# A hybrid decoder layer: half of the second output projection placed beside attention, attention's outputs loaded in 4 pieces, fill-in steps tied to an issue order

## The chip, the cores and the metric

One core of a Trainium2 chip runs the whole layer in one launch. The metric is device microseconds per execution. Engines are TensorE (PE in the profile), VectorE (DVE), ScalarE (ACT), GpSimd (POOL) and SyncE (SP), whose queue issues nearly all transfers.

## The reference

A batch of 1, 1024 tokens, 1024 channels, all in float32. The layer is a half-step SwiGLU network, a mixer, and a second half-step network, each between two RMS norms:

```python
h = h + 0.5 * rms_norm(swiglu(rms_norm(h, ffn1_pre_g), ...), ffn1_post_g)
m = hybrid_mixer(rms_norm(h, mix_pre_g), ...)
h = h + rms_norm(m, mix_post_g)
h = h + 0.5 * rms_norm(swiglu(rms_norm(h, ffn2_pre_g), ...), ffn2_post_g)

# in hybrid_mixer:
attn = nsa_attention(q, k_cmp, v_cmp, k_sel, v_sel, k_win, v_win, gates)   # T x 512
lru = rg_lru(xr, xg, conv_w, conv_b, lru_w_a, ...)                          # T x 512
y = jnp.concatenate([rms_norm(attn, attn_out_g), rms_norm(lru, lru_out_g)], axis=-1)
return y @ w_out                                                            # 1024 x 1024
```

The two networks have 2816 hidden channels. Attention has 8 query heads of 64 channels and three branches: compressed blocks, selected blocks (16 of at most 16, so all) and a window of 512. The recurrence has 512 channels.

## The kernel before

**Products.** Each float32 product is made as three rounded ones (`mm3`, lines 152 to 156): both operands are split into a rounded part and a remainder (`split`, L133 and L134; with a gain per channel L136 and L137), and TensorE runs high by high, high by low and low by high. A product of 128 x 512 is so three matmuls. A split operand of the network is called a hat (`xh`), of the output projection `yh`, of a weight `wh`.

**Stages.** Tokens are worked in two halves of 512. The first network comes first, then the mixer's input projections that attention of half 0 (tokens 0 to 511) needs, then that attention, beside which the other projections of half 1 and the recurrence are computed; then attention of half 1, beside which half 0 gets its output projection, its residual and the first hats of the second network; then, with nothing of attention left, the output projection of half 1, its residual, the rest of the hats, and the second network. The second network multiplies by a 2 x 2 block scheme with seven products, of which products 1 and 2 need half 0 alone. They can be made ahead for up to 11 tiles of hidden channels: `F2.early()`, 11 x 4 products of 12 matmuls, called early products here, whose results go to DRAM.

**Attention.** One unit is one head and 256 queries, 16 units in each half. `front` loads Q from DRAM, makes the scores, adds the distance penalty on VectorE (L1087), exponentials on ScalarE, scaling by gates on GpSimd. `back` transposes the probabilities, splits them and multiplies by the values; the 128 x 256 result is copied by ScalarE and stored (L1157, L1158). A unit's back is emitted two units after its front (SKEW), and `merge` weaves the steps of front, back and a filler in proportion to their counts, with at most QUOTA filler steps per unit (8 in the first attention, 15 in the second).

**The output projection** has two groups of 512 input channels: group 0 is attention's, group 1 the recurrence's. `out_rows` loads a group's 4 tiles (y), for group 0 adds the two halves of each on GpSimd (L1186), splits them with their gain and sums the squares. `out_group` loads the weights and makes 8 outputs of 128 x 512 from 12 matmuls each, 96 a group; the first group writes the scaled product into `m` (L1221), the second adds to it (L1223).

**The order.** The program text is not the issue order: a list scheduler, with its own cost figures, chooses for each engine among the instructions that are ready. The text, buffer counts and explicit ties (`issue_after`) bound what it may do. SP's queue issues strictly in its order.

**After attention of half 1** group 1 comes first with 5 early steps after each of its 4 tiles, then group 0 with 2 after each; then residual, 12 early steps, reload of half 0's parts (L309), and `build1` with 2 early steps after each hat.

Of the kernel before, what the change touches and what calls it, by code (L numbers as in the profile page):

```python
# [8 lines left out]
F32 = mybir.dt.float32  # L9
# [3 lines left out]
OP = mybir.AluOpType  # L13
# [7 lines left out]
NH = 8  # L21
# [15 lines left out]
SLOW = 8, 6  # L37
BESIDE = dict(rows=5, more=2, res=12, hats=2)
XS, CA, HX = 3, 3, 8
# [7 lines left out]
def layer(ctx: ExitStack, tc: tile.TileContext, I: dict, out: bass.AP):  # L47
# [181 lines left out]
    class Ffn:  # L229
# [12 lines left out]
        def open_outputs(self):  # L242
            self.ws, self.ap = (pool(self.sap, n + self.name, side="right") for n in ("ws", "ap"))

# [217 lines left out]
        def hidden(self):  # L462

            self.at = pool(self.sap, "at" + self.name)
            last = iter(())
            for f in range(NP):
                S = {}
                for m in range(2):
                    u = self.unit(f, m, S, (f, m) == (NP - 1, 1))
                    next(u)  # L470
                    run(last)
                    next(u)
                    last = u
            run(last)
# [177 lines left out]
    dq = [[dram.tile([128, 2, HT], F32, name=f"dq{h}{c}") for c in range(4)] for h in range(2)]  # L652
    dy = [[dram.tile([8, 128, 256], F32, name=f"dy{h}{pr}") for pr in range(2)] for h in range(2)]
    dl = [dram.tile([512, HT], F32, name=f"dl{h}") for h in range(2)]
# [464 lines left out]
    def back(ap, u):  # L1119
# [8 lines left out]
        def values(wi, runs, PT, npart):  # L1128
            at = 0
            for ri, (br, j, k0, nk) in enumerate(runs):  # L1130
                lhs = V[:, j, br - 1, g] if br else VC[:, g]
                for y in range(2):
                    nc.tensor.matmul(av[:, k0 * 128:(k0 + nk) * 128], lhs, PT[:npart, y, at:at + nk * 128],
                                     start=(wi == 0 and y == 0),
                                     stop=(wi == len(work) - 1 and ri == len(runs) - 1 and y == 1))
                at += nk * 128
# [20 lines left out]
        nc.scalar.activation(o, av[:, :256], AF.Copy)  # L1157
        nc.sync.dma_start(dy[h][pr][hd], o)  # L1158

    def attention(ap, units, filler, quota):  # L1160
        for n in range(len(units) + SKEW):
# [4 lines left out]
            if n >= SKEW:  # L1166
                u = units[n - SKEW]
                gens.append((back(ap, u), len(pieces(u["at"][0] * 4 + u["at"][2] * 2))))
            gens.append((filler, quota, True))
            merge(*gens)  # L1170
# [3 lines left out]

    def out_rows(tile_for, h, grp):

        ys = []
        sq = tile_for("sq", [128, HT], F32)
        for f in range(4):
            y = tile_for("y", [128, 2, HT], F32)  # L1180
            if grp == 0:
                for pr in range(2):
                    for e in range(2):
                        nc.sync.dma_start(y[e * 64:(e + 1) * 64, :, pr * 256:(pr + 1) * 256],
                                          dy[h][pr][2 * f + e].rearrange("(j d) t -> d j t", j=2))
                nc.gpsimd.tensor_tensor(y[:, 0], y[:, 0], y[:, 1], op=OP.add)  # L1186
# [12 lines left out]

    def out_group(ys, sq, grp, m, first, tag="pj", done=lambda: None):  # L1200

        ps = ptile(tag)
        for t in range(4):
            nc.tensor.matmul(ps[:, t:t + 1], sq[:, t * 128:(t + 1) * 128], ones, start=True, stop=True)
        ssb = stat("ssb", (128, 4))
        nc.vector.tensor_copy(ssb, ps[:, :4])
        rs = [rsqrt_mean(ssb[:, t:t + 1], 512) for t in range(4)]
        for dh in range(2):
# [5 lines left out]
            for t in range(4):  # L1214
                p = ptile("pj")
                for f in range(4):
                    mm3(p, cols(ys[f], t), (w[f][:, 0], w[f][:, 1]), f == 0, f == 3)
                    yield
                d = m[t][:, dh * 512:(dh + 1) * 512]
                if first:  # L1220
                    nc.scalar.activation(d, p, AF.Copy, scale=rs[t])  # L1221
                else:
                    nc.vector.scalar_tensor_tensor(d, p, rs[t], d, op0=OP.mult, op1=OP.add)  # L1223
                if dh:
                    done()

    sat0, sat1, som, soy, sm0 = (ExitStack() for _ in range(5))
    ap = pool(sat0, "at0", side="right")
# [24 lines left out]
    def in_hats(kind, shape, dt):  # L1253
# [3 lines left out]
        return F2.xa.tile(shape, dt, name=kind, tag=tag)  # L1257

    def beside_attention():
        for grp in (1, 0):  # L1260
            ys, sq = yield from out_rows(in_hats, 0, grp)
            for _ in range(IDLE):
                yield
            yield from out_group(ys, sq, grp, m0, grp == 1)
        yield from slow(res(0, m0), SLOW[0])
# [3 lines left out]
        som.close()  # L1269
        F2.open_outputs()  # L1270
        yield from early

    early = F2.early()
    beside = beside_attention()
    attention(ap, [{"at": (1, hd, pr)} for hd in range(NH) for pr in range(2)], beside, QUOTA[1])
    sat1.close()
# [6 lines left out]
    oy = pool(soy, "oy")  # L1283

    def in_own(kind, shape, dt):
        return oy.tile(shape, dt, name=kind, bufs=dict(yh=8, y=4, sq=2)[kind])

# [9 lines left out]

    F2.tags = ("sc",)
    group1 = out_group(*go(out_rows(in_own, 1, 1), BESIDE["rows"]), 1, m1, True, "pt")
    next(group1)  # L1300
    rows = go(out_rows(in_own, 1, 0), BESIDE["more"])
    run(group1)
    last = res(1, m1)
    run(out_group(*rows, 0, m1, False, "pt", lambda: next(last)))
    run(last)
# [4 lines left out]
    F2.open_parts()  # L1310
    F2.reload()
    F2.ttags = ("pt", "pj")
# [35 lines left out]
```

## Time and profile before

| | |
|---|---|
| three timed runs | 1997.56, 1989.90, 1991.17 us; median 1991.17 |
| the profiled execution | 1994.11 us, span 1992.3 us |
| TensorE busy | 1905.8 us, 96% |
| VectorE, ScalarE, GpSimd busy | 1374.9, 980.3, 567.4 us |
| mean granted clock of TensorE | 0.983 |

The mixer's attention of half 0 lies between 877 and 1047 us, that of half 1 between 1047 and 1339; the end of the output projection and the residual follow until 1455, and the second network after it. Busy time is an average over stages: TensorE's 96% leaves 86 us in which it is idle, and the lower clock at some places adds to what is lost. A matmul's duration in the timeline overlaps its neighbours, so the pitch from start to start is read.

### The profile page before, as it was taken

What the parts mean: (1) busy time and instruction counts of PE and PEld (TensorE: products, weight loads), DVE (VectorE), ACT (ScalarE), POOL (GpSimd) and SP (SyncE); (2) the same over time, 40 slices, a digit from 0 to 9 for tenths busy, and PEclk for the clock granted to TensorE, in tenths of its full rate; (3) what the DMA queues carried; (4) which work ended last, traced back from release to release, by engine and by line L of the source; (5) the groups of instructions that cost most, each with busy time, mean ns of one, the idle gap of its engine ahead of it and who ended that gap; (6) DMA issues with size and microseconds to landing.
All of it is one profiled execution on the core that took longest, in us unless ns stands there. A gap on an engine that the chain in (4) does not pass through costs nothing. (4 is left out here: it accounts for less than half of the span.)

```text
span 1992.3 us, 26839 instructions
## 1 busy us (share of the span) xinstructions
PE 1905.8 (96%) x9034; PEld 1561.8 (78%) x9034; DVE 1374.9 (69%) x2509; ACT 980.3 (49%) x1895; POOL 567.4 (28%) x549
## 2 busy tenths in 40 slices
PE   7999999999999989899999989988989999999998
PEld 6788888887787866688787878877868888888876
DVE  5877766657677745856885785654788766767776
ACT  7432333334446656558786686754733322334353
POOL 1432222110021444255434331213243333210211
PEclk9999999999999999899999999998989999999999
DMA  7555333348767543562323253224755555568654
GB/s 222 169 164 164 112 101 116 101 149 274 246 197 238 163 135 101 154 172 78 130 86 115 82 171 117 72 87 146 233 160 177 167 172 178 176 229 310 202 190 184
DMA packets 292699, 320.73 MB, mean 161 GB/s; under 512 B 19696, under 2 KB 200016, under 8 KB 292560
## 3 DMA queue, kind: packets, MB, share of 16 engines
q1 hardware_dynamic: 291984, 316.91, 49.8%
q0 software_dynamic: 576, 2.10, 0.4%
q8 instruction: 71, 1.16, 0.2%
q14 instruction: 68, 0.56, 0.1%
HBM read 237.62 MB, written 79.17 MB: 159 GB/s over the span
## 5 line engine op out<-in xcount | busy, mean ns | idle before, releaser
L133 ACT ACTIVATE wh<-ws 128x512 fp32r<-128x512 f32 x242 | 150.6, 626 | 270.3 <-PE pb L156 159.4
L154 PE MATMUL pb<-xh,wh 128*128 128x512 f32 x600 | 234.8, 394 | 5.1 <-ACT wh L133 3.8
L134 DVE TENSOR_TENSOR wh<-wr,wh 128x512 fp32r<-128x512 f32 (+1 forms) x243 | 183.6, 761 | 76.9 <-ACT wh L133 74.2
L155 PE MATMUL pb<-xh,wh 128*128 128x512 f32 x600 | 235.9, 393 | 0.4 <-DVE xh L134 0.4
L156 PE MATMUL pb<-xh,wh 128*128 128x512 f32 x600 | 231.9, 393 | 2.7 <-DVE wh L134 2.7
L133 ACT ACTIVATE wh<-wr 128x512 fp32r<-128x512 f32 (+1 forms) x243 | 150.0, 623 | 170.4 <-PE pb L156 80.1
L134 DVE TENSOR_TENSOR wh<-ws,wh 128x512 fp32r<-128x512 f32 x242 | 184.0, 762 | 9.6 <-ACT wh L133 7.9
L133 ACT ACTIVATE wh<-hx 128x512 fp32r<-128x512 f32 x149 | 93.8, 630 | 195.6 <-PE pb L156 105.0
L154 PE MATMUL pa<-xh,wh 128*128 128x512 f32 x456 | 178.6, 392 | 1.0 <-ACT wh L133 0.7
L342 POOL TENSOR_TENSOR ws<-wr 128x512 f32<-128x512 f32 x55 | 75.6, 1376 | 361.4 <-DVE wh L134 258.6
L155 PE MATMUL pa<-xh,wh 128*128 128x512 f32 x456 | 178.1, 391 | 0.0
L156 PE MATMUL pa<-xh,wh 128*128 128x512 f32 x456 | 175.9, 391 | 1.2 <-DVE wh L134 1.2
L1100 POOL TENSOR_SCALAR s<-s,cf 128x64 f32<-128x64 f32 (+4 forms) x192 | 115.9, 625 | 185.6 <-DVE cf L1096 152.9
L134 DVE TENSOR_TENSOR wh<-hx,wh 128x512 fp32r<-128x512 f32 x149 | 104.9, 704 | 68.5 <-ACT wh L133 68.2
L144 POOL TENSOR_TENSOR wh<-wr,wh 128x512 fp32r<-128x512 f32 (+1 forms) x74 | 102.2, 1392 | 142.9 <-ACT wh L143 113.8
L154 PEld LDWEIGHTS pb<-xh,wh 128*128 128x128 f32 x600 | 113.6, 189 | 30.4 <-ACT wh L133 4.3
L155 PE MATMUL pa<-wh 128*128 128x512 f32 x332 | 131.4, 396 | 5.3 <-DVE wh L134 2.8
L156 PEld LDWEIGHTS pb<-xh,wh 128*128 128x128 f32 x600 | 113.4, 189 | 28.3 <-DVE wh L134 3.9
L155 PEld LDWEIGHTS pb<-xh,wh 128*128 128x128 f32 x600 | 113.5, 189 | 25.1 <-DVE xh L134 0.8
L154 PE MATMUL pj<-xT,wh 128*128 128x512 f32 (+1 forms) x304 | 123.6, 410 | 8.9 <-DVE gq L941 5.2
L156 PE MATMUL pa<-wh 128*128 128x512 f32 x332 | 130.3, 393 | 0.0
L134 DVE TENSOR_TENSOR PT<-pt,PT 128x512 fp32r<-128x512 f32 (+3 forms) x184 | 104.1, 578 | 28.0 <-ACT PT L133 27.4
(372 smaller groups left out, 4671.0 us busy)
## 6 DMA issues: line engine op xcount, KB each, us to landing
hx<-hid SPq DMA_DIRECT2D x154, 256.0 KB
wr<-in_ffn_w_down SPq DMA_DIRECT2D x63, 512.0 KB
wr<-in_ffn_w_gate SPq DMA_DIRECT2D x60, 512.0 KB
wr<-in_ffn_w_up SPq DMA_DIRECT2D x60, 512.0 KB
hid<-S SPq DMA_DIRECT2D x104, 256.0 KB
wr<-in_ffn_w_down SPq DMA_DIRECT2D x72, 256.0 KB
wr<-in_w_in SPq DMA_DIRECT2D x36, 512.0 KB
hid<-s SPq DMA_DIRECT2D x66, 256.0 KB
```

Source lines behind the costliest of these rows:

```text
L133: nc.scalar.activation(hi, src, AF.Copy)
L134: tt(lo, src, hi.bitcast(F32), op=OP.subtract)
L144: nc.gpsimd.tensor_tensor(lo, src, hi.bitcast(F32), op=OP.subtract)
L154: nc.tensor.matmul(p, a[0], b[0], start=start and fresh, stop=False, skip_group_check=not fresh)
L155: nc.tensor.matmul(p, a[0], b[1], start=False, stop=False, skip_group_check=not fresh)
L156: nc.tensor.matmul(p, a[1], b[0], start=False, stop=stop, skip_group_check=not fresh)
L342: (nc.vector if turn[0] % every == 0 else nc.gpsimd).tensor_tensor(s, a, b, op=op)
L1100: nc.gpsimd.tensor_scalar(S[k, br][:, :n], S[k, br][:, :n], cf[:, k, br:br + 1], 1.0, op0=OP.mult, op1=OP.mult)
```

## The change

The recurrence's group of half 1 is computed beside attention of half 1, as one more part of the filler: its own pool, 18 early steps, then the products, each copied with its scale by ScalarE to a tile and stored to DRAM (`aside`, 8 stores of 256 KB to `dm`). After attention they are read back as rows of `m1` by 4 loads of 512 KB, and group 0 is added to them.

Attention's outputs are kept in DRAM in the layout in which they are read. A unit stores them in two pieces of 64 x 256; a group's 4 tiles are read by 4 loads of 512 KB where 16 loads of 128 KB stood. After attention those loads stand first, and the reloads of `m1` and of half 0's parts are tied behind the last of them.

The filler's steps are tied (`behind`): those emitted in one iteration may not be issued before the last value product of the unit before the one whose back is emitted there. In the last two iterations the quota is doubled. 18 early steps are tied behind attention's very last value product; after the residual 16 early steps stand where 12 stood, and 3 after each hat where 2 stood. The sum of squares is made after a group's first product, not ahead of it, and a pool of the second network is opened later.

```diff
 SLOW = 8, 6
-BESIDE = dict(rows=5, more=2, res=12, hats=2)
+BESIDE = dict(rows=18, res=16, hats=3)
 XS, CA, HX = 3, 3, 8
...
         def open_outputs(self):
-            self.ws, self.ap = (pool(self.sap, n + self.name, side="right") for n in ("ws", "ap"))
+            self.ap = pool(self.sap, "ap" + self.name, side="right")
+
+        def open_sums(self):
+            self.ws = pool(self.sap, "ws" + self.name, side="right")
 
...
 
+            self.open_sums()
             self.at = pool(self.sap, "at" + self.name)
...
     dq = [[dram.tile([128, 2, HT], F32, name=f"dq{h}{c}") for c in range(4)] for h in range(2)]
-    dy = [[dram.tile([8, 128, 256], F32, name=f"dy{h}{pr}") for pr in range(2)] for h in range(2)]
+    dy = [[dram.tile([2, 64, 2, HT], F32, name=f"dy{h}{f}") for f in range(4)] for h in range(2)]
+    dm = [dram.tile([128, D], F32, name=f"dm{t}") for t in range(4)]
     dl = [dram.tile([512, HT], F32, name=f"dl{h}") for h in range(2)]
...
                 for y in range(2):
-                    nc.tensor.matmul(av[:, k0 * 128:(k0 + nk) * 128], lhs, PT[:npart, y, at:at + nk * 128],
-                                     start=(wi == 0 and y == 0),
-                                     stop=(wi == len(work) - 1 and ri == len(runs) - 1 and y == 1))
+                    u["last"] = nc.tensor.matmul(av[:, k0 * 128:(k0 + nk) * 128], lhs, PT[:npart, y, at:at + nk * 128],
+                                                 start=(wi == 0 and y == 0),
+                                                 stop=(wi == len(work) - 1 and ri == len(runs) - 1 and y == 1))
                 at += nk * 128
...
         nc.scalar.activation(o, av[:, :256], AF.Copy)
-        nc.sync.dma_start(dy[h][pr][hd], o)
+        for j in range(2):
+            nc.sync.dma_start(dy[h][hd // 2][hd % 2, :, j, pr * 256:(pr + 1) * 256], o[j * 64:(j + 1) * 64])
+
+    def behind(last, gen):
+
+        while True:
+            with tc.issue_after(last.ins):
+                try:
+                    next(gen)
+                except StopIteration:
+                    return
+            yield
 
...
                 gens.append((back(ap, u), len(pieces(u["at"][0] * 4 + u["at"][2] * 2))))
-            gens.append((filler, quota, True))
+            most = quota if n < len(units) else 2 * quota
+            gens.append((behind(units[n - SKEW - 1]["last"], filler) if n > SKEW else filler, most, True))
             merge(*gens)
...
 
-    def out_rows(tile_for, h, grp):
+    def load_y(y, h, f):
+        return nc.sync.dma_start(y, dy[h][f].rearrange("e d j t -> (e d) j t"))
+
+    def out_rows(tile_for, h, grp, loaded=None):
 
...
         for f in range(4):
-            y = tile_for("y", [128, 2, HT], F32)
+            y = loaded[f] if loaded else tile_for("y", [128, 2 - grp, HT], F32)
             if grp == 0:
-                for pr in range(2):
-                    for e in range(2):
-                        nc.sync.dma_start(y[e * 64:(e + 1) * 64, :, pr * 256:(pr + 1) * 256],
-                                          dy[h][pr][2 * f + e].rearrange("(j d) t -> d j t", j=2))
+                if not loaded:
+                    load_y(y, h, f)
                 nc.gpsimd.tensor_tensor(y[:, 0], y[:, 0], y[:, 1], op=OP.add)
...
 
-    def out_group(ys, sq, grp, m, first, tag="pj", done=lambda: None):
-
-        ps = ptile(tag)
-        for t in range(4):
-            nc.tensor.matmul(ps[:, t:t + 1], sq[:, t * 128:(t + 1) * 128], ones, start=True, stop=True)
-        ssb = stat("ssb", (128, 4))
-        nc.vector.tensor_copy(ssb, ps[:, :4])
-        rs = [rsqrt_mean(ssb[:, t:t + 1], 512) for t in range(4)]
+    def out_group(ys, sq, grp, put, tag="pj"):
+
+        rs = []
         for dh in range(2):
...
                     yield
-                d = m[t][:, dh * 512:(dh + 1) * 512]
-                if first:
-                    nc.scalar.activation(d, p, AF.Copy, scale=rs[t])
-                else:
-                    nc.vector.scalar_tensor_tensor(d, p, rs[t], d, op0=OP.mult, op1=OP.add)
-                if dh:
-                    done()
-
-    sat0, sat1, som, soy, sm0 = (ExitStack() for _ in range(5))
+                if not rs:
+                    ps = ptile(tag)
+                    for i in range(4):
+                        nc.tensor.matmul(ps[:, i:i + 1], sq[:, i * 128:(i + 1) * 128], ones, start=True, stop=True)
+                    ssb = stat("ssb", (128, 4))
+                    nc.vector.tensor_copy(ssb, ps[:, :4])
+                    rs = [rsqrt_mean(ssb[:, i:i + 1], 512) for i in range(4)]
+                put(t, dh, p, rs[t])
+
+    def onto(m, first, done=lambda: None):
+
+        def put(t, dh, p, r):
+            d = m[t][:, dh * 512:(dh + 1) * 512]
+            if first:
+                nc.scalar.activation(d, p, AF.Copy, scale=r)
+            else:
+                nc.vector.scalar_tensor_tensor(d, p, r, d, op0=OP.mult, op1=OP.add)
+            if dh:
+                done()
+        return put
+
+    def aside(t, dh, p, r):
+
+        o = F2.keep("ca", CA)
+        nc.scalar.activation(o, p, AF.Copy, scale=r)
+        nc.sync.dma_start(dm[t][:, dh * 512:(dh + 1) * 512], o)
+
+    sat0, sat1, som, soy, sm0, so1 = (ExitStack() for _ in range(6))
     ap = pool(sat0, "at0", side="right")
...
 
+    def in_own(pl, yhs):
+        return lambda kind, shape, dt: pl.tile(shape, dt, name=kind, bufs=dict(yh=yhs, y=2, sq=1)[kind])
+
+    def some(gen, n):
+        for _ in range(n):
+            next(gen, None)
+            yield
+
     def beside_attention():
...
                 yield
-            yield from out_group(ys, sq, grp, m0, grp == 1)
+            yield from out_group(ys, sq, grp, onto(m0, grp == 1))
         yield from slow(res(0, m0), SLOW[0])
...
         F2.open_outputs()
+        ys, sq = yield from out_rows(in_own(pool(so1, "o1", side="right"), 4), 1, 1)
+        yield from some(early, 18)
+        yield from out_group(ys, sq, 1, aside)
+        so1.close()
         yield from early
...
     beside = beside_attention()
-    attention(ap, [{"at": (1, hd, pr)} for hd in range(NH) for pr in range(2)], beside, QUOTA[1])
+    units = [{"at": (1, hd, pr)} for hd in range(NH) for pr in range(2)]
+    attention(ap, units, beside, QUOTA[1])
     sat1.close()
...
     oy = pool(soy, "oy")
-
-    def in_own(kind, shape, dt):
-        return oy.tile(shape, dt, name=kind, bufs=dict(yh=8, y=4, sq=2)[kind])
 
...
     F2.tags = ("sc",)
-    group1 = out_group(*go(out_rows(in_own, 1, 1), BESIDE["rows"]), 1, m1, True, "pt")
-    next(group1)
-    rows = go(out_rows(in_own, 1, 0), BESIDE["more"])
-    run(group1)
+    ys = [oy.tile([128, 2, HT], F32, name="y", bufs=4) for _ in range(4)]
+    landed = [load_y(ys[f], 1, f) for f in range(4)][-1]
+    with tc.issue_after(landed.ins):
+        for t in range(4):
+            nc.sync.dma_start(m1[t], dm[t])
+    with tc.issue_after(units[-1]["last"].ins):
+        for _ in range(BESIDE["rows"]):
+            next(beside)
+    rows = run(out_rows(in_own(oy, 4), 1, 0, ys))
     last = res(1, m1)
-    run(out_group(*rows, 0, m1, False, "pt", lambda: next(last)))
+    run(out_group(*rows, 0, onto(m1, False, lambda: next(last)), "pt"))
     run(last)
...
     F2.open_parts()
-    F2.reload()
+    with tc.issue_after(landed.ins):
+        F2.reload()
     F2.ttags = ("pt", "pj")
```

What the scheduler makes of it at three places. First TensorE at the end of the second attention; `av` are the value products, `pj<-wh,yh` the output projection, `sc<-xh,wh` and `pj<-xh,wh` early products. Before:

```order
L1133 MATMUL av<-PT,V 128x256 x4
L1146 MATMUL pt<-idt,s_12559 128x128
L1133 MATMUL av<-PT,V 128x256 x5
L1133 MATMUL av<-PT,V 128x128 x6
L154 MATMUL pj<-wh,yh 128x512
L155 MATMUL pj<-wh,yh 128x512
L154 MATMUL pj<-wh,yh 128x512
```

Behind the last value product stand the 192 matmuls of the projection. In the changed kernel:

```order
L156 MATMUL pj<-xh_3_11704,wh 128x512
L1138 MATMUL av<-PT,V 128x256 x2
L1138 MATMUL av<-PT,V 128x128 x6
L154 MATMUL sc<-xh_0_11268,wh 128x512
L155 MATMUL sc<-xh_0_11268,wh 128x512
L156 MATMUL sc<-xh_0_11268,wh 128x512
L154 MATMUL sc<-xh_1_11424,wh 128x512
L155 MATMUL sc<-xh_1_11424,wh 128x512
L156 MATMUL sc<-xh_1_11424,wh 128x512
L154 MATMUL sc<-xh_2_11551,wh 128x512
```

48 early matmuls stand behind the last value product, then the 96 of group 0; the 96 of the recurrence's group stand in the units before.

SP's queue at the same place. `dy` holds attention's outputs, `dl` the recurrence's, `dm` the stored products, `h` the residual, `wr` weights. Before:

```order
L1158 DMA dy_92<-avo 128x256
L1158 DMA dy_93<-avo 128x256
L1188 DMA y<-dl_95 128x512 x4
L178 DMA xres<-h_80 128x1024 x3
L1184 DMA y<-dy_92 64x2x256 x2
L1184 DMA y<-dy_93 64x2x256 x2
```

The last two rows repeat three times more. In the changed kernel:

```order
L1164 DMA dy_97<-avo 64x256 x2
L1225 DMA wr<-in_w_out 128x2x512
L1193 DMA y<-dy_94 128x1024
L1193 DMA y<-dy_95 128x1024
L1193 DMA y<-dy_96 128x1024
L1193 DMA y<-dy_97 128x1024
L1345 DMA xrow<-dm_98 128x1024
```

Attention's loads follow the last store with one weight load between; the loads of the recurrence's y and three of the residual's are gone from there, and loads of `dm` stand behind.

SP's queue where the first attention passes into the second. `dq_86` are the queries of the second half's first heads, `dy_90`, `dy_91` (before) and `dy_93` (after) the first attention's outputs. Before:

```order
L1158 DMA dy_90<-avo 128x256
L1064 DMA Q<-dq_85 64x2x256 x2
L931 DMA dl_95<-lr 128x512
L1064 DMA Q<-dq_86 64x2x256 x5
L1158 DMA dy_91<-avo 128x256
L1064 DMA Q<-dq_85 64x2x256 x2
L1064 DMA Q<-dq_86 64x2x256
L1158 DMA dy_90<-avo 128x256
L1158 DMA dy_91<-avo 128x256
```

Five loads of the second attention's queries stand ahead of the last stores of the first. In the changed kernel:

```order
L1164 DMA dy_93<-avo 64x256 x2
L1225 DMA wr<-in_w_out 128x2x512
L936 DMA dl_103<-lr 128x512
L1069 DMA Q<-dq_86 64x2x256
L1164 DMA dy_93<-avo 64x256 x2
L1069 DMA Q<-dq_86 64x2x256 x2
L1206 DMA y<-dl_102 128x512 x2
L1069 DMA Q<-dq_86 64x2x256 x3
```

Queries are loaded around the last store, one ahead of it and the others behind, and the loads of half 0's recurrence lie between them.

On TensorE, the second attention's units with no or few fill-in matmuls are, numbered from 0 to 15, before the units 5, 11, 12 and 15; in the changed kernel the units 4 to 10. In the first attention fill-in stands before in units 0 to 7, and in the changed kernel in 14 of the 16, mostly 24 matmuls each. In the changed kernel units 14 and 15 of the second attention have 78 early matmuls each, and the recurrence's group is in units 12 and 13. The early products between the last transposes and the first product of the network's main part number 83 before and 143 in the changed kernel.

## Rows read from the trace of the kernel before

**Rows 1.** Busy by stretch (stretch; its length, each engine's busy us, clock, DMA share, GB/s).
```profile
1047.00:1339.00 292.00, 278.18 (x1650) 233.22 (x1647) 197.71 (x534) 201.14 (x424) 89.71 (x115) 0.99 0.34 105
1339.00:1370.00 31.00, 20.70 (x77) 16.51 (x78) 12.02 (x22) 14.82 (x25) 17.01 (x16) 0.72 0.57 175
1455.00:1475.00 20.00, 13.09 (x42) 9.39 (x41) 19.77 (x23) 7.24 (x13) 11.68 (x8) 0.74 0.70 221
```

**Rows 2.** Timeline, TensorE (start, us, instruction, idle before and releaser), end of attention.
```profile
1337.97 1.00 PE L1133 MATMUL av<-PT,V 128*128 128x256 f32 x7 [0.20 <-DVE PT L134]
...
1343.24 0.79 PE L154 MATMUL pj<-wh,yh 128*128 128x512 f32 x1 [4.27 <-ACT yh L136]
...
1351.20 1.05 PE L1204 MATMUL pt<-ones,sq 128*128 128x1 f32 x8 [0.54 <-POOL sq L1195]
...
1357.78 0.80 PE L154 MATMUL pj<-wh,yh 128*128 128x512 f32 x1 [5.52 <-ACT xrow L1221]
...
1371.06 0.39 PE L156 MATMUL pj<-wh,yh 128*128 128x512 f32 x1
...
1390.33 0.39 PE L154 MATMUL pj<-wh,yh 128*128 128x512 f32 x1
```

**Rows 3.** Timeline, SP's queue, the same place.
```profile
1339.79 1.87 SPq L1188 DMA_DIRECT2D y<-dl  x4
1341.76 1.32 SPq L178 DMA_DIRECT2D xres<-h  x3
1344.04 14.34 SPq L1184 DMA_DIRECT2D y<-dy  x16
```

**Rows 4.** Timeline, GpSimd, the same place: attention's y.
```profile
1354.62 1.26 POOL L1186 TENSOR_TENSOR y<-y 128x512 f32<-128x512 f32 x1 [3.47 <-DMA y<-dy]
...
1358.31 4.20 POOL L1186 TENSOR_TENSOR y<-y 128x512 f32<-128x512 f32 x3
```

**Rows 5.** Timeline, several engines, the second FFN's first products.
```profile
1456.42 0.68 DVE L134 TENSOR_TENSOR wh<-wr,wh 128x512 fp32r<-128x512 f32 x1
...
1456.63 1.62 POOL L342 TENSOR_TENSOR ws<-wr,ws 128x512 f32<-128x512 f32 x1 [1.88 <-DVE wh L134]
...
1457.02 1.77 DVE L257 TENSOR_TENSOR xs<-xp,xs 128x512 f32<-128x512 f32 x1
...
1459.45 0.50 PE L155 MATMUL pb<-xh,wh 128*128 128x512 f32 x1 [0.36 <-DVE xh L134]
...
1464.03 0.79 PE L154 MATMUL pb<-xh,wh 128*128 128x512 f32 x1 [3.84 <-ACT wh L133]
...
1467.95 0.80 PE L156 MATMUL pb<-xh,wh 128*128 128x512 f32 x1 [2.70 <-DVE wh L134]
```

**Rows 6.** Busy by stretch: units of attention (columns as in rows 1).
```profile
895.60:999.40 103.80, 99.72 (x540) 83.61 (x540) 75.01 (x203) 80.83 (x188) 49.74 (x66) 0.97 0.33 105
999.40:1046.70 47.30, 46.25 (x323) 40.42 (x322) 42.16 (x173) 43.12 (x138) 19.91 (x44) 1.00 0.28 84
1046.70:1070.00 23.30, 18.95 (x118) 15.85 (x117) 18.87 (x48) 17.18 (x39) 12.54 (x15) 0.93 0.55 165
1124.00:1172.00 48.00, 43.14 (x254) 35.10 (x252) 40.32 (x99) 36.41 (x75) 12.31 (x16) 1.00 0.41 132
1218.70:1263.90 45.20, 45.20 (x254) 38.04 (x254) 27.07 (x67) 29.12 (x58) 8.68 (x12) 1.00 0.38 123
1279.00:1301.30 22.30, 21.82 (x155) 19.11 (x154) 18.92 (x68) 16.91 (x41) 8.79 (x15) 1.00 0.04 13
```

**Rows 7.** Busy of one tile's instructions by stretch: xT, yh, xh.
```profile
895.60:999.40 103.80, 64.63 (x239) 43.66 (x238) 0.00 (x0) 0.00 (x0) 0.97 0.33 105
...
1124.00:1172.00 48.00, 18.51 (x72) 12.88 (x72) 0.00 (x0) 0.00 (x0) 1.00 0.41 132
...
1218.70:1263.90 45.20, 28.81 (x112) 20.21 (x112) 0.00 (x0) 0.00 (x0) 1.00 0.38 123
```

**Rows 8.** Groups of instructions, VectorE, 1047 to 1339 (busy, mean ns; idle before, releasers).
```profile
L1087 DVE CUSTOM_DVE_ANT_0 s<-sc,DW 128x512 f32<-128x512 f32 x28 | 19.2, 687 | 10.4 <-PE pt L1146 5.9 <-PE sc L1084 4.3
```

## The prediction

> **What bounds the kernel now.** I read the busy shares first (TensorE 1905.8 us of a span of 1992.3, 96%), then the busy time by stretches, the places where TensorE waits in its timeline, and single pairs of attention units. TensorE is the bound nearly everywhere, and the change takes no product away, so the time can only move where TensorE stands still or runs at its lower clock. Warm, a 512-column product follows the one before it after (1390.33 − 1371.06)/85 = 0.2267 us [rows 2]. Three stretches matter.
>
> At the end of attention, 1339 to 1370, the granted clock is 0.72 and TensorE is busy 20.70 of 31.00 us with 77 products [rows 1]. 61 of these are wide, 61 × 0.2267 = 13.8 us; the 16 narrow ones take about 2.0, twice the 1.05 of the row at 1351.20 [rows 2]. Lost: 31.0 − 13.8 − 2.0 = 15.2 us. The rows name the waits: 4.27 us for the first rounded copy of the recurrence's y, 0.54 for the sum of squares, 5.52 for attention's y [rows 2], 10.3 together; the rest, 4.9, is the lower clock of the two restarts. The cause of the longest wait stands on SP: the 16 loads of attention's outputs are issued from 1344.04 for 14.34 us, behind the recurrence's loads and the residual's [rows 3]; GpSimd adds the first pair at 1354.62 and the other three end at 1362.5 [rows 4].
>
> Late, 1455 to 1475, TensorE is busy 13.09 of 20 us at clock 0.74 and VectorE 19.77 [rows 1]: the second FFN's first products wait for copies that VectorE makes. 42 products × 0.2267 = 9.5, so about 10.5 us are lost, 0.36 + 3.84 + 2.70 = 6.9 of them standing [rows 5].
>
> In attention beside the output projection, 1047 to 1339, 278.18 of 292.00 us are busy, VectorE 197.71 [rows 1]. What a stretch costs there depends on what is filled in. A pair of units with 112 early products takes 45.20 us, less 112 × 0.2267 = 25.4: 19.8 net. A bare pair takes 22.30, 2.5 more. The pair with residual and transposes takes 48.00 with 72 projection products (16.3): 31.7 net, 11.9 more than a filled one [rows 6, 7].
>
> **The change, part by part.**
>
> *Term 1, the end of attention.* The recurrence's group (96 products and its loads) leaves this place; 48 early products of the second FFN, pinned behind attention's last product, stand first instead, 48 × 0.2267 = 10.9 us that need nothing from attention. SP issues 4 loads of attention's outputs at once after the last store, where 4 + 3 + 16 stood. All of the 15.2 goes if the first y's copies are ready within 10.9 us of the last product. Before, 4.27 us passed from there to the first product on a plainly loaded y [rows 2]; the new first y needs one add more, 1.26 [rows 4], and the fourth three adds after it, some 4.2: about 4.3 + 1.3 + 4.2 = 9.8 us, an estimate from these rows, with twice the bytes in each load. The three early loads don't wait for the last store, so I take it that one microsecond or so is left: **−14**. Bounds: −15.2, and, if the adds end 18.5 us after the first issue as they do now (1362.5 − 1344.04), 18.5 − 10.9 = 7.6 is left: −7.6. The reload of the recurrence's rows (4 loads of 512 KB) stands behind attention's loads and is wanted only when the first product of group 0 is summed; I cost it at nothing, under the same 10.9 us plus a row's 12 products (2.7). The same goes for the 18 steps' own weights: they are loaded beside attention.
>
> *Term 2, the late stall.* Between the last transposes and the FFN's first product the kernel now has 143 early products where it had 83: 60 × 0.2267 = 13.6 us more cover. VectorE, which is full there, must split 60/12 = 5 more weight tiles: 0.68 us each when GpSimd is quiet, 1.77 when it runs an add of its own [rows 5]. So VectorE's last copy comes 3.4 to 8.9 us later and TensorE 13.6: net 4.7 to 10.2 of the 10.5. I take **−7**, the middle; bounds −10.2 and 0 (if the copies wait on something that the new order also delays).
>
> Of these two prices, the row at 1457.02 (1.77 us, beside a GpSimd add from 1456.63) stands against the row at 1456.42 (0.68) [rows 5]. The Trainium skill, page "SBUF — State Buffer", section "SBUF: two separate sides", says that VectorE with two SBUF inputs and a reading GpSimd share a port pair as an exclusive lock: the one that comes second waits the whole instruction. By it every split that meets an add would pay the high price, and the term would be −4.7; without it −10.2.
>
> *Term 3, what attention gives back.* The recurrence's products now fill attention, and fill-in steps are tied to the last value product of the unit before the one being finished. This moves three things, and no row of before shows it, so I bound each.
> (i) In the new order the early products come at the end (78 in each of the last two units), the recurrence's in units 12 and 13 (from 0 to 15), and units 4 to 10, three to three and a half pairs, are bare or nearly so; before there are about two bare pairs. One and a half pairs × 2.5 = 3.7: **+3**.
> (ii) Residual and transposes fall into these bare pairs. Their work on VectorE is 40.32 − 18.92 = 21.4 us above a bare pair's [rows 6]; a bare pair has 22.30 − 18.92 = 3.4 us of VectorE free, three have 10.2; 21.4 − 10.2 = 11.2, against 11.9 that one pair pays now: **0**.
> (iii) At the seam between the two attentions, 1046.7 to 1070.0, TensorE now loses 23.30 − 18.95 = 4.35 us and some 7% of clock, 6 in all [rows 6]. In the new order Q's loads for the second attention stand behind the first one's last store, and 44 score products in a row follow. About 3 us for the load, by the 4.27 above less the copy; then 22 score pieces on VectorE at 0.687 [rows 8], 15.1 us, against some 8 us of products: 10 in place of 6: **+4**; bounds 0 and +9.
> (iv) In the first attention the fill-in is spread over nearly all units, where now units 0 to 7 carry it and 8 to 15 are bare. The seven filled ones after the first take 103.80 us with 239 wide products (54.2): 7.1 net each; the bare ones 47.30/8 = 5.9 [rows 6, 7]. If all 16 cost 7.1, +9.6; if all cost 5.9, −8.4. The recurrence's scan, which has no products of its own, has nothing beside it that fills: **+3**.
> Sum **+10**; ends −10 and +30, the upper one with every mishap at once.
>
> *At nothing:* the store of attention's outputs in two halves and the recurrence's rows through memory (8 stores, 4 loads of SP's queue, beside attention with its DMA share of 0.34 [rows 1]); if that cover fails, it shows as a later y in term 1. The sum of squares after the first product removes the 0.54 counted in term 1. ScalarE has the 8 scaled copies that it had before.
>
> Sum: −14 − 7 + 10 = −11. The profiled execution took 1994.1 us (span 1992.3 and 1.8 around it): 1983.1. The median of the three timed runs, 1991.2, lies 2.9 below the profiled one, so I forecast **1980**.
>
> **The rivals.**
> *Attention gives nothing back.* The pins give a steadier mix, (iv) pays for (i) and (iii). For it: bare units cost little, 5.9 against 7.1. Against: three bare pairs in a row. −14 − 7 = −21: 1970.
> *The late stall stays.* VectorE is busy 19.77 of 20 us there [rows 1]; if the five splits and the FFN's own land in front of the last copies, the cover is used up by what it brings. −14 + 10 = −4: 1987.
> *The cover at the end of attention is too short.* Attention's y arrive as late as now: −7.6 − 7 + 10 = −4.6: 1986 to 1987.
> *Slower: the bare pairs are bound by VectorE and ScalarE.* Residual and transposes sit in three pairs without products to hide them, and each pays what the one pays now: 3 × 11.9 − 11.9 = +24, with the seam's 4 and the 6 of (i) and (iv) +34 in place of +10: −14 − 7 + 34 = +13: 2004. For it: the dear pair pays 11.9 although it has 72 products to fill with; those are gone. At +21 the whole gain is eaten; from +31 on the kernel is slower by 0.5%. Against: the VectorE sum under (ii).
> That pins hold fill-in back from a stalled TensorE is the same rival in another place and has its chance there.
>
> **How the numbers follow.** Forecast (its own range 1975 to 1986) 0.38; nothing given back 0.24; late stall stays 0.13; short cover 0.09; slower 0.16. About 0.5%, 10 us, is what a measurement of this kernel can tell from no change: under 1981.2 is faster, over 2001.1 slower. Faster: two thirds of the forecast, 0.25, the 0.24, and 0.01 of the others: 0.50. Slower: most of the last, 0.14. Within: 0.36. The range leaves out a tenth on either side: 1965, where nothing is given back and both gains are whole (−15.2 − 10.2 = −25.4: 1965.8), to 2001.
>
> **What would show it.** Term 1: after the last value product some 48 early products at the high clock, then the projection with no wait over 2 us. Term 2: VectorE's last copy before TensorE's first FFN product, no wait for it over 3 us. Term 3: in the second attention the net time of bare pairs near 22 us (the forecast) or near 32 (the slower rival), a gap at the seam of about 10 us, first attention within a few us of now. Wrong if attention as a whole grows by over 30 us or shrinks at all, or if a wait over 5 us stands at either of the two mended places.

## The result and the profile after

The changed kernel is slower: 2016.72 us (median of five, 2012.62 to 2018.41) against 1992.01, ratio 1.0121 with a 95% interval of 1.0107 to 1.0136. Of the five runs of the kernel before, one of 4797.12 us is a slow one and stands outside the ratio. The forecast was 1980, 1965 to 2001.

The busy times of the changed kernel by stretch, as in [rows 1, 6] (stretch; length, then TensorE, its weight loads, VectorE, ScalarE, GpSimd; granted clock, DMA share, GB/s):

```profile
942.20:992.90 50.70, 42.08 (x207) 33.84 (x206) 31.59 (x90) 44.01 (x97) 22.54 (x30) 0.83 0.24 74
1051.50:1097.50 46.00, 39.36 (x178) 31.81 (x178) 26.54 (x94) 28.52 (x66) 20.82 (x27) 0.81 0.33 105
1097.50:1373.20 275.70, 260.54 (x1542) 217.02 (x1542) 184.62 (x502) 180.55 (x394) 81.45 (x104) 0.99 0.33 107
1373.20:1403.20 30.00, 25.60 (x107) 20.18 (x106) 14.04 (x21) 11.55 (x21) 12.95 (x11) 0.94 0.75 267
1473.00:1493.00 20.00, 17.56 (x74) 13.38 (x73) 14.46 (x18) 6.27 (x13) 8.00 (x7) 1.00 0.67 209
```

The two places that the change was meant to mend are mended in part: after attention the clock is 0.94 where it was 0.72, and the late stretch has 17.56 of 20 us busy where it had 13.09 [rows 1]. New are the first two rows: 51 us within the first attention at clock 0.83, and the first unit of the second attention, 46 us long at 0.81, where the seam had 0.93 [rows 6].

To compare stages I subtract from each stretch its matmuls at their warm pitch (0.227 us for 512 columns, 0.173 for 384, 0.116 for 256, 0.109 for 128, 0.05 for 64, each read where TensorE ran back to back); what is left is lost. All kernels here have the same 9034 matmuls, so the differences between them hang little on these pitches. Profiled executions, us lost, beside the median of all runs; the seam is the second attention's first unit, from the copy that ends the first attention to its own:

| kernel | median | 1st attention | seam | rest of 2nd | 30 us after | 90 to 150 us after |
|---|---|---|---|---|---|---|
| before | 1992.0 | 24.5 | 4.9 | 35.2 | 15.5 | 11.5 |
| changed | 2016.7 | 44.6 | 18.2 | 41.5 | 7.2 | 3.8 |
| e1 ties beside 2nd only | 1977.3 | 24.6 | 1.1 | 43.0 | 7.7 | 4.7 |
| e2 no ties | 1972.6 | 23.0 | 1.1 | 36.5 | 7.4 | 4.0 |
| e3 before, ties beside 1st | 2030.4 | 44.3 | 18.8 | 41.9 | 15.7 | 11.1 |
| e4 quota 16 | 1986.1 | 30.8 | 1.1 | 45.7 | 9.2 | 5.8 |
| e5 no ties, 30 steps | 1974.2 | 21.5 | 1.1 | 41.8 | 0.8 | 10.1 |
| e6 no ties, 12 and 2 | 1975.1 | 22.9 | 1.1 | 35.9 | 7.7 | 5.8 |
| e7 no ties, 0 steps | 1992.9 | 21.6 | 1.1 | 40.5 | 20.6 | 9.2 |
| e8 looser ties | 1995.2 | 40.7 | 6.6 | 35.5 | 7.4 | 5.1 |
| e9 | 1966.7 | 24.5 | 1.1 | 37.7 | 0.8 | 4.2 |
| e9b | 1963.6 | 21.6 | 1.1 | 41.1 | 0.8 | 3.1 |
| e10 before, 4 loads | 1991.3 | 21.6 | 2.3 | 42.2 | 14.6 | 12.1 |
| e11 ties in 1st half of 1st | 1986.9 | 31.1 | 3.6 | 40.9 | 8.3 | 6.0 |

From before to changed: +20.1 + 13.3 + 6.3 − 8.3 − 7.7 = +23.7. The two profiled executions, 1994.1 and 2012.6 us, lie only 18.5 apart; the missing 5 are won in the first network (last section), and that the sum comes near the 24.7 between the medians is chance. One execution carries noise: e2, e5, e6 and e7 issue the same instructions in the same order in both attentions up to the last units, and the column "rest of 2nd" still runs from 35.9 to 41.8. Its +6.3 proves nothing; the +20 and the +13 stand far outside.

**The seam.** Timeline of the changed kernel, TensorE and SP, where the first attention ends:

```profile
1049.09 2.41 PE L1138 MATMUL av<-PT,V 128*128 128x256 f32 x11
1049.27 0.34 SPq L936 DMA_DIRECT2D dl<-lr  x1
1049.66 0.56 SPq L1069 DMA_DIRECT2D Q<-dq  x1
1051.95 1.10 SPq L1164 DMA_DIRECT2D dy<-avo  x2
1053.10 1.23 SPq L1069 DMA_DIRECT2D Q<-dq  x2
1055.88 0.42 PE L1088 MATMUL sc<-KC,Q 128*128 128x64 f32 x1 [4.37 <-DMA Q<-dq]
```

The recurrence's last store (`dl<-lr`) is issued at 1049.27, and the second attention's first query load right behind it. A unit's queries come in two loads; the other is issued at 1053.10, behind the store of the first attention's last output, and TensorE waits 4.37 us for the two. Then it has scores with few fill-in products between them, 42 and 12 matmuls in the first 20 us:

```profile
1051.50:1071.50 20.00, 13.89 (x55) 10.55 (x54) 12.74 (x44) 12.54 (x29) 2.65 (x3) 0.83 0.56 178
1071.50:1097.50 26.00, 25.47 (x125) 21.26 (x125) 13.80 (x51) 15.98 (x37) 18.16 (x25) 0.80 0.15 48
```

Of the 18.2 us lost, TensorE stands 6.6; most of the rest is the clock, which is low in these 26 us too, where TensorE is busy 25.47. In the kernel before, five of these loads stand ahead of the first attention's last stores, as the order of SP's queue shows. The second attention's tiles are opened in the program only after those of the recurrence are closed; whether the place in the queue or that memory holds the loads back is not separated.

**The first attention.** The dear place is the recurrence's `scan`: large activations with their tables on ScalarE, then four scans on VectorE. The four units around it (3 to 6 before, 7 to 10 in the changed kernel), first the busy times, then the fill-in matmuls alone (tile xT). Before:

```profile
918.60:982.50 63.90, 59.82 (x308) 49.34 (x307) 44.63 (x112) 52.96 (x117) 32.49 (x41) 0.95 0.36 117
...
918.60:982.50 63.90, 40.98 (x149) 27.93 (x149) 0.00 (x0) 0.00 (x0) 0.95 0.36 117
```

Changed (its busy times together are the first row of this section; here in three parts, then the fill-in):

```profile
942.20:961.90 19.70, 18.12 (x86) 14.84 (x85) 7.01 (x26) 17.83 (x35) 9.04 (x14) 0.84 0.29 88
961.90:979.60 17.70, 14.79 (x86) 12.33 (x85) 14.03 (x45) 17.56 (x49) 8.74 (x12) 0.89 0.28 90
979.60:992.90 13.30, 9.17 (x38) 6.67 (x37) 10.56 (x20) 8.62 (x17) 4.76 (x6) 0.75 0.12 31
...
942.20:992.90 50.70, 14.37 (x47) 9.98 (x46) 0.00 (x0) 0.00 (x0) 0.83 0.24 74
```

In the changed kernel ScalarE is busy 35.39 of the first 37.40 us; in the last 13.30 it is not, and there TensorE's two longest waits, 1.93 and 1.69 us, end on VectorE, which runs the scans. So these two engines set the length of the stretch with few products beside it. Before, 149 fill-in matmuls lie in it, and ScalarE is busy 52.96 of 63.90; in the changed kernel 47, the others being tied to other units. Less the fill-in at 0.2267 us the stretches cost 63.9 − 33.8 = 30.1 and 50.7 − 10.7 = 40.0 us: 10 of the 20 lost. The other 10 are spread, the most of them on the first unit, which has no fill-in now (some 3), and on the last (some 3).

### The profile page after: what moved, and what is told of

Its sections match the earlier page's. It is cut to its first block, busy times and chain, and to the rows that moved or that the text cites. A ratio compares the mean times of both kernels' runs of the same rounds, so it can differ in the third digit from the quotient of the medians.

```text
span 2010.8 us, 26804 instructions
## 1 busy us (share of the span) xinstructions
PE 1923.4 (96%) x9034; PEld 1568.4 (78%) x9034; DVE 1383.8 (69%) x2509; ACT 970.9 (48%) x1887; POOL 579.4 (29%) x549
## 5 line engine op out<-in xcount | busy, mean ns | idle before, releaser
L134 DVE TENSOR_TENSOR wh<-wr,wh 128x512 fp32r<-128x512 f32 (+1 forms) x243 | 190.8, 790 | 75.2 <-ACT wh L133 72.4
```

The lines of the kernel that those rows point to most:

```text
L134: tt(lo, src, hi.bitcast(F32), op=OP.subtract)
```

## The experiments

Theory A: the ties beside the first attention are the loss, by the place to which they put the fill-in. Theory B: the forecast's slower rival, the bare units of the second attention. A tie orders TensorE's instructions alone; what depends on a tied product moves with it.

**e1, ties beside the second attention only.**

```diff
-            gens.append((behind(units[n - SKEW - 1]["last"], filler) if n > SKEW else filler, most, True))
+            gens.append((behind(units[n - SKEW - 1]["last"], filler) if n > SKEW and units[0]["at"][0] == 1 else filler, most, True))
```

> The changed kernel, with its filler's ties kept beside the second attention alone. Theory A (the ties beside the first attention are the loss: they hold projections and recurrence back into its last units, +20 us there, and the recurrence's late end holds the second attention's queries, +13 at the seam): the issue order of the first attention is that of the kernel before again, 33 us come back, 1980 to 1987 us, and the seam's first unit takes about 14 us instead of 46. Theory B (the forecast's slower rival: the bare units of the second attention are the loss): 2005 to 2015.

Measured 1977.3 us, ratio to before 0.9932 (0.9918 to 0.9946): 39 us come back, more than the 33 of A, and B is far off. The seam's unit:

```profile
1039.90:1051.40 11.50, 11.36 (x78) 9.74 (x76) 9.80 (x32) 9.99 (x27) 5.42 (x9) 1.00 0.73 222
```

B falls with it, since from its unit 6 on the second attention carries fill-in as in the changed kernel.

**e2, no ties.**

```diff
-            gens.append((behind(units[n - SKEW - 1]["last"], filler) if n > SKEW else filler, most, True))
+            gens.append((filler, most, True))
```

> The changed kernel without any tie of the filler (the 18 early steps behind attention's last product stay). Theory A: like the kernel with ties beside the second attention, 1980 to 1987 us; the ties there are worth under 4 us either way, since the bare units only move from the middle to the end. Theory B: if ties make the bare units that cost, this one is some 10 us faster than the kernel with ties beside the second attention.

1972.6 us, 0.9924 (0.9904 to 0.9943); its runs spread from 1964.8 to 1981.0, and the interval overlaps that of e1. Whether the ties beside the second attention cost or give anything is not separated.

**e3, the kernel before with ties beside the first attention:** `behind` and `u["last"]` as in the change, and

```diff
-            gens.append((filler, quota, True))
+            gens.append((behind(units[n - SKEW - 1]["last"], filler) if n > SKEW and units[0]["at"][0] == 0 else filler, quota, True))
```

> The kernel before, with the ties beside the first attention added and nothing else. Theory A: this alone costs 25 to 35 us, 2017 to 2027, with the seam's first unit at 40 us or more. Theory B: within 10 us of the kernel before, under 2002.

2030.4 us, 1.0199 (1.0186 to 1.0213): 40 us slower by this part alone, more than the 25 to 35 that A gave. The same seam, TensorE and SP:

```profile
1053.63 0.38 SPq L931 DMA_DIRECT2D dl<-lr  x1
...
1055.02 2.51 SPq L1064 DMA_DIRECT2D Q<-dq  x4
...
1060.03 0.39 PE L1083 MATMUL sc<-KC,Q 128*128 128x64 f32 x1 [7.25 <-DMA Q<-dq]
```

**e4, all ties, more steps per unit:** `QUOTA = 16, 15`.

> The changed kernel with all its ties, and 16 filler steps per unit of the first attention instead of 8, so that the tied steps are through by unit 7 as in the kernel before. Theory A in its narrow form (where the ties put the fill-in costs, not the ties): 1981 to 1990 us. If the tie itself costs (TensorE stands though fill-in is ready), it stays over 2000.

1986.1 us, 0.9985 (0.9971 to 0.9998): 30 of the 39 us come back with every tie in place, so the place is most of it. The seam is whole (1.1). In the first attention 6 us more than in e1 stay lost, 4 of them in one unit of the scan, which has 34 fill-in matmuls where e1 has 55 (e4 busy, e4 fill-in, e1 fill-in); net of them it costs 14.7 us against 10.7, with ScalarE busy 22.19 of 22.40:

```profile
917.30:939.70 22.40, 19.66 (x92) 16.34 (x91) 10.18 (x29) 22.19 (x42) 10.74 (x11) 0.85 0.30 92
...
917.30:939.70 22.40, 9.61 (x34) 7.61 (x35) 0.00 (x0) 0.00 (x0) 0.85 0.30 92
...
911.70:934.90 23.20, 14.72 (x55) 10.02 (x55) 0.00 (x0) 0.00 (x0) 1.00 0.34 97
```

**e8, looser ties:** `units[n - SKEW - 4]["last"]` with `n > SKEW + 3`.

> The changed kernel with its ties three units looser (behind the value products of the fourth unit before the one being finished), 8 steps per unit as before. The fill-in now ends in unit 12 of the first attention. Theory A in its narrow form (the place costs): about half of the loss stays, 1990 to 2003 us: the scan's ScalarE work in units 5 to 7 still has 0 to 18 matmuls beside it, and the seam's queries come earlier than in the changed kernel. If the tight tie itself is what costs, 1975 to 1985.

1995.2 us, 1.0021 (1.0007 to 1.0035). The fill-in ends in unit 12, and the seam loses 6.6; the scan's stretch has 48 fill-in matmuls, the clock is 0.74, and 52.4 − 10.9 = 41.5 us are left:

```profile
935.30:987.70 52.40, 41.87 (x196) 34.59 (x195) 32.19 (x96) 40.07 (x95) 22.68 (x33) 0.74 0.23 69
...
935.30:987.70 52.40, 13.27 (x48) 8.63 (x46) 0.00 (x0) 0.00 (x0) 0.74 0.23 69
```

**e11, ties in the first 9 iterations of the first attention** (and all of the second): `if n > SKEW and (h or n < 9)`, with h the token half. The fill-in ends in unit 11, about as in e8, but the scan's stretch has its products:

> The changed kernel with the ties beside the first attention in its first 9 iterations only. The fill-in ends in unit 11, much as with the looser ties (unit 12, 1995 us), but the stretch in which the recurrence keeps ScalarE busy has 47, 20 and 62 matmuls beside it again instead of 18, 0 and 12. If products missing beside ScalarE's work are what the first attention loses, and the late end what the seam loses, both are nearly gone: 1977 to 1985 us. If any tie or any late end costs, 1990 to 2000.

```profile
942.20:1010.20 68.00, 62.89 (x323) 51.76 (x322) 47.16 (x119) 55.06 (x120) 29.87 (x39) 0.95 0.35 109
...
942.20:1010.20 68.00, 43.21 (x158) 29.42 (x158) 0.00 (x0) 0.00 (x0) 0.95 0.35 109
```

1986.9 us, 0.9983 (0.9972 to 0.9995), 2 us above what A gave. Less its fill-in, 68.0 − 35.8 = 32.2 us, the stretch costs nearly what it did before (30.1). The seam lost 3.6. So both causes are shown: products missing beside the scan, and the late end of the fill-in, with which the seam's loss goes (18.2 where it ends in unit 15, 6.6 in unit 12, 3.6 in unit 11, 1.1 in unit 7). Some 9 us above e1 remain here and in e4. In e11 they are 2.5 at the seam and 6.5 in the first attention, about 3 of these in its first unit, which has 3 fill-in matmuls where e1 has 50; the rest is not explained.

**e6, fewer steps around the last hats:** e2 with `res=12, hats=2`.

> The kernel without ties, with 12 and 2 early steps around the residual and the last hats, as in the kernel before, instead of 16 and 3. If the shorter late stall (3 to 4 us lost where the kernel before loses 11) comes from these numbers, it is back: 6 to 8 us slower, 1979 to 1981. If it comes from the early products that the 18 steps and the moved group left over, no change within 2 us.

1975.1 us, 0.9914 (0.9899 to 0.9929): no change that can be measured. 143 early products still lie between the last transposes and the network's first product, as in e2.

**e7, no step behind attention's end:** e2 with `rows=0`.

> The kernel without ties, and no early step behind attention's last product: the projection's first product waits for attention's loads with nothing in front. If the gain at the end of attention is the cover of these 48 matmuls (10.9 us), the loss there goes from 7.4 to 14 to 18 us, and the kernel is 7 to 10 us slower, 1980 to 1983. If the four early loads are the gain, it changes by under 3 us.

1992.9 us, 1.0006 (0.9996 to 1.0016): 20 us slower, twice what was expected. TensorE:

```profile
1341.77 0.80 PE L154 MATMUL pj<-wh,yh 128*128 128x512 f32 x1 [7.67 <-ACT yh L136]
...
1446.42 0.77 PE L154 MATMUL sc<-xh,wh 128*128 128x512 f32 x1 [5.83 <-DVE S L380]
```

The first wait is the uncovered load of attention's y. The second was not foreseen: the steps now stand late, where an early product itself waits until VectorE has read out an earlier one.

**e5, 30 steps behind attention's end:** e2 with `rows=30`.

> The kernel without ties of the filler, with 30 early steps behind attention's last product instead of 18 (79 matmuls ahead of the projection instead of 48). The end of attention still loses about 7.5 us there (waits of 0.9, 1.6 and 1.9 us for the last copies and for the sums of squares, and the clock after them). If these waits are a matter of cover, 31 x 0.227 = 7 us more of it takes 4 to 6 us off, 1967 to 1969 us against some 1973. If they are a chain behind the first product (both psum tiles wait for the sums' scale), under 2 us come off.

1974.2 us, 0.9914 (0.9902 to 0.9926). The end of attention is cured (0.8 us lost, no wait), so that was cover; but the total stands, for the late stall is back:

```profile
1444.32 0.80 PE L154 MATMUL pb<-xh,wh 128*128 128x512 f32 x1 [4.85 <-ACT wh L133]
1446.67 0.80 PE L156 MATMUL pb<-xh,wh 128*128 128x512 f32 x1 [1.14 <-DVE wh L134]
```

Only 95 early products are left between the last transposes and the first network product. Both waits draw on one stock: 228 early products were left after attention before, some 323 in e2, e5 and e6.

**e9 and e9b, a larger stock:** e5 with `most = quota` in attention's last iterations; e9b also with `QUOTA = 8, 14`.

> The kernel without ties, with 30 early steps behind attention's last product and no doubled quota in attention's last two iterations, so that 78 early matmuls more are left for the place after attention and units 12 to 15 are bare. If the waits at the end of attention and before the second network share one stock of early products (with 30 steps the first is cured, and the second is back), a larger stock cures both: 5 to 8 us lost in all instead of 11, 1967 to 1970 us. If the bare units at the end of attention charge for it (2 more bare pairs at up to 2.5 us each), 1972 to 1975, no gain.

> The same with 14 instead of 15 filler steps per unit, so some 50 early matmuls more after attention, and units 11 to 15 bare. By the stock: no further gain once both waits are gone, 1967 to 1970 us; by the price of bare units 1 to 3 us slower than the kernel with 15.

1966.7 us, 0.9878 (0.9857 to 0.9898), and 1963.6, 0.9869 (0.9848 to 0.9891). These beat both kernels; between the two the intervals overlap, and the price that both expectations feared for more bare units does not show. In e9 the 30 us after attention have no idle time:

```profile
1313.10:1343.10 30.00, 30.00 (x134) 24.24 (x134) 15.97 (x23) 14.74 (x25) 13.04 (x11) 1.00 0.77 276
```

**e10, the kernel before with two stores a unit and 4 loads of 512 KB in place of 16**, in the old order.

> The kernel before with the new layout of attention's outputs alone: two stores a unit, 4 loads of 512 KB instead of 16 of 128 KB, in the old order behind the recurrence's and the residual's loads; no tie, no group moved. The 5.5 us wait for attention's y and the slow clock after it should go, 4 to 8 us, 1983 to 1987 us; the first wait (4.3 us) and the late stall stay. If the loads were not what held it, no change within 2 us.

1991.3 us, 1.0003 (0.999 to 1.0015): no change, against what was expected. The loads are issued in half the time (7.46 us, where 16 took 14.34 [rows 3]), and the second wait shrinks from 5.52 to 3.35, but the first grows from 4.27 to 5.31 [rows 2]:

```profile
1341.42 0.79 PE L154 MATMUL pj<-wh,yh 128*128 128x512 f32 x1 [5.31 <-ACT yh L136]
...
1354.14 0.69 PE L154 MATMUL pj<-wh,yh 128*128 128x512 f32 x1 [3.35 <-ACT xrow L1219]
```

## Why the prediction was wrong

The mark set for being wrong was met: both attentions together grew by 39.7 us, over the 30.

**The step that failed** is (iv) of term 3, +3 with an end of +9.6: it measured +20. It priced the first attention's units at their net cost, 5.9 or 7.1 us, as if fill-in were worth the same beside any unit. It never asked which engine bounds the stretch that the fill-in leaves: beside the scan that is ScalarE, then VectorE. ScalarE is busy 52.96 of 63.90 us in four of the seven filled units; the row over all seven, 80.83 of 103.80 [rows 6], has it too but was read for its net time alone. e11 against e8 shows it, for 9 of the 20 us; the rest of the 20 lies in the first and last units and is in part only located. The recurrence's scan, which "has nothing beside it that fills", was named and taken as small.

**(iii), the seam,** was seen in the order and mis-sized: +4, ends 0 and +9, measured +13. The load's wait, about 3 us in the forecast, was 4.37. What was left out is the clock, 0.81 over the 46 us of the unit, and that the place hangs on the late end of the fill-in and the recurrence: e4, where it ends in unit 7, loses 1.1. The 44 scores do not stand in a row either; the trace has fill-in products among them.

**(i) and (ii), the bare units:** +3 forecast; +6.3 in one execution, within the spread of equal kernels. The slower rival had the direction but not the place. The sentence behind it, on pins that hold fill-in back from a stalled TensorE, comes nearest to what happened, but it was given no price of its own. Two bare pairs of the changed kernel's second attention, the second with transposes:

```profile
1186.00:1206.30 20.30, 19.16 (x137) 16.42 (x137) 16.78 (x57) 14.86 (x40) 6.56 (x9) 1.00 0.15 40
...
1219.80:1247.80 28.00, 24.53 (x171) 20.61 (x169) 26.00 (x71) 23.56 (x55) 9.68 (x11) 1.00 0.33 113
```

20 to 28 us, not the 32 that the rival needs for each.

**Term 1** was −14 and measured −8.3, near its upper bound of −7.6. The mechanism held: 48 early products run at the full clock. The size was off, since the last copies are not ready 9.8 us after the last value product but some 17: GpSimd's first add starts 7 us after it, and copies, adds and squares follow on three engines. TensorE, GpSimd and VectorE in the changed kernel:

```profile
1371.98 1.01 PE L1138 MATMUL av<-PT,V 128*128 128x256 f32 x8
...
1380.04 1.28 POOL L1204 TENSOR_TENSOR y<-y 128x512 f32<-128x512 f32 x1 [50.65 <-PE pj L156]
...
1388.78 0.73 PE L156 MATMUL pj<-wh,yh 128*128 128x512 f32 x2 [0.89 <-DVE yh L137]
...
1389.25 0.74 DVE L137 SCALAR_TENSOR_TENSOR yh<-y,par,yh 128x512 fp32r<-128x512 f32 x1
...
1392.53 1.05 PE L1235 MATMUL pt<-ones,sq 128*128 128x1 f32 x8 [1.64 <-POOL sq L1213]
...
1395.45 0.50 PE L154 MATMUL pj<-wh,yh 128*128 128x512 f32 x1 [1.87 <-DVE xrow L1248]
```

e5 shows that 30 steps cover it: 60 products ahead of the projection's first, and some 20 more among its first 16. That the four loads would be a gain of their own is refuted by e10, and e7, which has them first and no cover, loses 20.6 us there, more than the kernel before.

**Term 2** was −7 and measured −7.7. The count was right (143 early products in place of 83). The forecast does not say where they come from; it isn't the larger step numbers, for e6 has the 143 without them. They come from the moved group, which displaces 95 early products from beside attention to after it. By the lock that the Trainium skill states ("SBUF — State Buffer", "SBUF: two separate sides") the term would have been −4.7, without it −10.2; −7.7 lies between, and no run here tells them apart.

Without the ties the change gives 0.76% (e2), some 15 us. That is near the forecast's second case, nothing given back and 21 won, but not by its parts: terms 1 and 2 give 8.1 and 7.5 in e2, the seam 3.8, and the first network, of which the forecast has no term, some 3 to 5 (last section). They add to more than 15, since the profiled execution of e2 is its fastest run; how the 15 of the median are shared is not shown.

## What to carry to other kernels

Before fill-in work is moved away from a place, look which engine bounds that place for itself: the stretch with the recurrence's work on ScalarE and VectorE took 149 matmuls and cost 10 us less, net of them, than with 47. A tie on one engine delays everything that depends on the tied work, to its last store and to the loads queued behind it; look at what ends last. Cover that serves two waits is one stock: curing one wait from it can bring back the other, and here a larger stock cured both.

## What the runs showed of the hardware

**A part of the change outside the forecast.** TensorE has the same order in the first 850 us in all kernels, but the pool that is opened later is opened in the first network too, and there VectorE, GpSimd and SP have another order from 424 us on. Between the same two matmuls of TensorE, 459 and 498 us in the kernel before, 5.4 us are lost in it, 2.7 in e3 and 3.1 in e10, which keep its pools, and 0.1 to 0.3 in the eleven kernels with the change's pools. Before, and changed:

```profile
455.00:498.00 43.00, 40.40 (x167) 31.93 (x167) 30.35 (x47) 18.70 (x34) 1.82 (x1) 0.96 0.82 280
...
455.00:493.00 38.00, 38.00 (x169) 31.21 (x168) 29.74 (x46) 19.03 (x34) 2.13 (x2) 1.00 0.93 335
```

So 3 to 5 us of the gain of e1, e2, e5, e6, e9 and e9b are probably this part's; no run takes it alone.

**Noise.** In the first 850 us these eleven kernels issue in one order and lost 58 to 63 us each, and six runs of e2 spread from 1964.8 to 1981.0 us. A single execution's total is therefore uncertain by 10 us and more here; stages beyond the first 850 us can be compared, totals only over several runs.
